# Layer A's attention of a two-layer diffusion trunk: three pairs of PSUM banks in turn, one bank for projections and one for values

## The chip, the cores and the metric

The kernel runs on one core of one Trainium2 chip. A core has a matrix engine (PE, with its weight loads PEld), three engines for elementwise work (DVE, ACT, POOL), a queue engine for transfers (SP), and PSUM, the memory that PE writes its results into: 8 banks of 512 float32 for each of the 128 partitions. A tile of 1024 float32 takes two banks, called a pair here. The metric is the device time of one execution in microseconds (us); lower is better.

## What is computed

Two layers over 1024 latent tokens (on a grid 64 wide) and 256 context tokens, each token a vector of 1024. The context tokens share the layer's weights. Layer 0 uses windowed attention with 16 query heads on 4 key heads of 64, a sink logit per head and a rotary embedding; layer 1 uses attention over a two-dimensional neighbourhood with a relative bias. Each has a gate path:

```python
for i in range(DEPTH):
    shift, scale, gate = split(silu(c) @ w_ada[i] + b_ada[i], 3)      # and the same for the context
    u  = h * (1 + scale) + shift
    uc = hc * (1 + scale_c) + shift_c
    if i == 0: y, yc = mixer_a(u, uc, ...)
    else:      y, yc = mixer_b(u, uc, ...)
    h = layer_norm(ALPHA * h + gate * y)          # hc likewise, after layer 0
# mixer_a
q, k, v, g = split(u @ w_in)                      # q, k rotated on the latent tokens
s_lat = where(|i - j| <= 128, q k^T / 8, -1e30)   # a block of 128 queries sees 3 blocks of keys
s_ctx = q kc^T / 8                                # and the 256 context keys
p = softmax([s_lat, s_ctx, sink])
y = ((p_lat v + p_ctx vc) * silu(g)) @ w_out
```

Context queries see the context keys only.

## The kernel before

Matrices are multiplied as 32-bit floats split into a high and a low part (three matmuls for a product). The program goes through layer A's modulated inputs, keys and values, then layer A's attention with its query and gate projections, the output projection and the layer norm, and then the same for layer B. The part that the change touches is layer A's attention.

**Sub-steps.** The 16 heads go in 8 pairs, p = 0 to 7. For each p there are 10 blocks b of 128 tokens (8 latent, 2 context) and two heads h: 160 sub-steps, k = 20p + 2b + h (`subsA`). Sub-step k computes its scores S_A (`qkA`, L694: PE L704 and L705, 640 columns for an inner block, 512 for blocks 0 and 7, 256 for the context blocks 8 and 9, each twice, with the high and the low part of the keys). DVE takes them out of PSUM with the mask and the row minimum (L317), POOL adds the sink (L322), ACT takes the exponent (L324). In the next sub-steps DVE takes the reciprocal of the sum (L328), POOL scales (L329), PE transposes the tile into T_A (L336, up to five times 128x128), ACT copies the high part out (L340) and DVE subtracts to get the low part (L342). After both heads of a block PE multiplies with the values into pvA (`pvA_fn`, L725, PE L733), first with the high part, one sub-step later with the low part; the result of two blocks stands in one bank, and after the second of them ACT (L742) and DVE (L743) take it out.

**Projections beside it.** While p is attended, the gates of p and the queries of p+1 are projected (`proj_pieces`, L190): for each of three chunks of tokens (512, 512 and 256) a tile pj of 24 matmuls (L208 to L210). A query chunk is taken out by DVE's shuffle (L469) and multiply by the cosine (L470), both of which read the bank, followed by POOL L471 and DVE L472 and by the copies L659 on ACT and L660 on DVE; the third chunk, of context tokens, goes to L659 and L660 at once. A gate chunk is taken out by ACT's tanh (L277) and DVE's L278. `merge` (L284) lays the two lists, attention and projection, into one another by their costs. DVE also works through products for the modulation of later stages (L611, L617).

**Order.** The framework builds each engine's order when the program is built, by simulating the engines: an instruction's priority is its place in the program, raised by `lift` for some (the eviction of the scores by 80, L342 by 60), and an instruction whose tile has no free bank is passed over until one is free. So the banks that a tile may take shape the order on all engines.

**Banks.** One pool for the whole kernel: two pairs (`psbig`, L97), which scores and transposes share, and four single banks (`psone`, L100), which all else shares: projections, values, transposes of the inputs, and the first output tiles yA0. A new tile waits until the last reader of the tile that held the bank has finished.

**The end of the stage.** In period p = 7 there are no further queries to project. In their place stand the splitting of the output weights and, from `og_first` on, the first output block's product into yA0, of two single banks. Behind the attention a loop over 10 blocks forms the output, the gate, the residual and the norm (L890).

Of the kernel before, what the change touches and what calls it, by code (L numbers as in the profile page):

```python
# [11 lines left out]
F32 = mybir.dt.float32  # L12
# [4 lines left out]
PSUM = bass.MemoryType.PSUM  # L17
DRAM = bass.MemoryType.DRAM

P = 128  # L20
# [62 lines left out]
def build(tc, i, out):  # L83
# [3 lines left out]
    es = ExitStack()  # L87
# [4 lines left out]
        return p, st  # L92

    dr = es.enter_context(tc.tile_pool(name="dr", bufs=1, space=DRAM))
    ps = es.enter_context(tc.tile_pool(name="ps", bufs=1, space=PSUM))

    def psbig(name):  # L97
        return ps.tile([P, 1024], F32, tag="big", bufs=2, name=name)

    def psone(name):  # L100
        return ps.tile([P, 512], F32, tag="one", bufs=4, name=name)

    cp = es.enter_context(tc.tile_pool(name="cp", bufs=1, side="left"))
    ident = cp.tile([P, P], F32, name="ident")
# [299 lines left out]
    HALVES = (slice(0, 512), slice(512, 1024))  # L404
# [239 lines left out]
    pp_st.close()  # L644
    pq, pq_st = pool("attA", "right")


    qA, gA, kA, vA = {}, {}, {}, {}

# [160 lines left out]
    for p in range(8):  # L810
        att = [x for row in rowsA[p * 20 : (p + 1) * 20] for x in row]
        if p % 2 == 0 and p:
            k_load(p // 2, 1)
        if p % 2 == 1 and p < 7:
            att.insert(20, (0.0, lambda p=p: k_load(p // 2 + 1, 0), 0))
            att.insert(24, (0.0, lambda p=p: v_loadA(p // 2 + 1), 0))
        if p < 7:
            n = len(att)
            for g in range(SEG[p]):
                att.insert(3 + g * (n // SEG[p] + 1), dots.pop(0))  # L820
            if not dots:
                att.append((0.0, dots_end, 0))
            merge(att, gprojA(p) + qprojA(p + 1), lead=0.0)
        else:

            att += [x for row in rowsA[8 * 20 :] for x in row]
            g7, fill = gprojA(7), []
            woA = OutWeights(up, "woA")
            for n, piece in enumerate(g7):
                fill.append(piece)  # L830
                if n >= 8:
                    fill.append((200.0, lambda j=n - 8: wo_piece(woA, i["wAo"], j)))
            assert len(fill) == G7_AT[2]
            oA0, yA0 = [], []

            def og_first():
                oA0.extend(og_small(og_load(0, 0)))
                yA0.extend(psone(f"yA0_{nh}") for nh in range(2))

            fill.append((0.0, og_first))  # L840
            for n in range(2 * KT):
                fill.append((300.0, lambda n=n: out_part(yA0, HALVES[n // KT], oA0, woA, (n % KT,))))
            merge(att[:-6], fill, lead=1500.0)
            gts = up.tile([P, 2, D], F32, tag="l2", bufs=1, name="gates")
            for v in range(2):
                gate_rows(gts[:, v], dcol[:, 0:8, v])
            raw = og_load(0, 1)
            merge(att[-6:], [])
# [42 lines left out]
    for b in range(10):  # L891
        z = oa.tile([P, D], F32, tag="z", bufs=2, name="z")
        dma(z, i["htok"][b])
        if b == 0:
            yh = yA0
        else:
            o = og_split(up, raw, "h2") if b % 2 else og_split(oa, raw, "og")
            if b < 9:
                raw = og_load(0, b + 1)
            y = psbig(f"yA{b}")  # L900
            yh = [y[:, sl] for sl in HALVES]
            for sl in HALVES:
                out_part(yh, sl, o, woA, range(KT))
        if pend is not None:
            u_from(*pend)
        g = gts[:, b // 8]
        for sl, yy in zip(HALVES, yh) if b == 0 else ((slice(0, D), y),):
            nc.vector.tensor_tensor(yy, yy, g[:, sl], ALU.mult)
            nc.vector.scalar_tensor_tensor(z[:, sl], z[:, sl], ALPHA, yy, ALU.mult, ALU.add)
        st = oa.tile([P, 2, 6], F32, tag="stat", bufs=2, name="stat")  # L910
        for nh in range(2):
            nc.vector.bn_stats(st[:, nh, :], z[:, HALVES[nh]])
        mv, rs = ln_stats(oa, st)
        nc.vector.scalar_tensor_tensor(rs[:, 0:1], mv[:, 0:1], -1.0, rs[:, 1:2], ALU.mult, ALU.mult)
        nc.scalar.activation(z, z, AF.Identity, bias=rs[:, 0:1], scale=rs[:, 1:2])
        if b < 8:
            dma(zdd[b * P : (b + 1) * P, :], z)
        pend = (b, z)

    def k_evac(dst, pl):  # L920
        def evac(pt, t0, n):
# [236 lines left out]
    def grid_rows(t, b):  # L1158

        return t.rearrange("(r c) d -> r c d", c=64)[:, 8 * b : 8 * b + 8, :]  # L1160
# [40 lines left out]
    for j in range(4):  # L1201
        t = ob.tile([P, D], F32, name=f"vec{j}")
# [4 lines left out]
    for b in range(8):  # L1207
        x = ob.tile([P, D], F32, tag="x", bufs=2, name="x")
        dma(x, grid_rows(zdd, b))  # L1209
        tok = slice(b * P, (b + 1) * P)  # L1210
        if 0 < b < 7:
            raw = og_load(1, b + 1, 7)
            on = og_split(ob, raw, "og") if b % 2 == 0 else og_split(ub, raw, "l2")
        nc.gpsimd.tensor_tensor(x, x, vecs[0], ALU.mult)  # L1214
        nc.gpsimd.tensor_tensor(x, x, vecs[1], ALU.add)  # L1215
        y = [y0, y1][b] if b < 2 else [psone(f"yB{b}_{nh}") for nh in range(3 if b == 7 else 2)]
        pairs = (o1 if b < 2 else o) + [(o7[:, 0, tok], o7[:, 1, tok])]

        cuts = (0, 512, 768, 1024) if b == 7 else (0, 512, D)
        parts = [slice(*c) for c in zip(cuts, cuts[1:])]  # L1220
        for sl in parts:
            out_part(y, sl, pairs, woB, range(KT) if b > 1 else (KT - 1,))
        if b:
            o = on
        if b == 0:
            g1 = ob.tile([P, D], F32, name="g1")
            gate_rows(g1, dcol[:, 24:32, 0])
        z = ob.tile([P, D], F32, tag="z", bufs=3, name="z")
        st = ob.tile([P, 3, 6], F32, tag="stat", bufs=2, name="stat")
        for j, sl in enumerate(parts):  # L1230
            nc.vector.tensor_tensor(z[:, sl], part_of(y, sl), g1[:, sl], ALU.mult)  # L1231
            nc.vector.tensor_tensor(z[:, sl], z[:, sl], x[:, sl], ALU.add)  # L1232
            nc.vector.bn_stats(st[:, j, :], z[:, sl])  # L1233
        mv, rs = ln_stats(ob, st[:, : len(parts)])
        cuts = (0, 512, 1024) if b == 7 else (0, D)
        parts = [slice(*c) for c in zip(cuts, cuts[1:])]
        for sl in parts:
            nc.vector.scalar_tensor_tensor(z[:, sl], z[:, sl], mv[:, 0:1], vecs[2][:, sl], ALU.subtract, ALU.mult)  # L1238
        for sl in parts:
            nc.vector.scalar_tensor_tensor(z[:, sl], z[:, sl], rs[:, 1:2], vecs[3][:, sl], ALU.mult, ALU.add)  # L1240
            dma(grid_rows(out, b)[:, :, sl], z[:, sl])
    ob_st.close()
    ub_st.close()
    wp_st.close()
# [94 lines left out]
```

## Time and profile before

| | |
|---|---|
| time, median of 3 runs | 1449.96 us (1449.54 to 1451.34) |
| time of the profiled execution | 1450.25 us |
| its span, first to last instruction | 1448.5 us |
| granted PE clock, mean | 0.994 |
| PE, DVE, ACT, POOL busy | 96%, 68%, 51%, 44% of the span |
| layer A's attention | about 97.8 to 590 us of the span |
| one p within it | about 60.7 us |

The profile is one execution taken by the hardware profiler. The profiled execution's own time is 1.75 us above its span. "L336" is a line of the kernel. In a list of waits, "PE T_A L336 <- DVE m_A L317" is time in which PE stood before a transpose until DVE had done its work at L317. A row of a timeline gives start, duration, engine, line, operation, and what is written from what is read; PE's matmuls are pipelined, so that a row's duration is longer than the distance to the next one.

### The profile page before, as it was taken

Reading aid. Unit: us, or ns where it says so; the run is one execution under the profiler, and the core shown is the slowest. Engines: PE = TensorE matmul, PEld = TensorE weight load, DVE = VectorE, ACT = ScalarE, POOL = GpSimd, SP = SyncE. Lnnn points to the kernel's source line nnn. Section 1 sums busy time; section 2 is a strip of 40 time slices with the busy share of each in tenths; the row PEclk is TensorE's granted clock in tenths of the full one; section 3 lists DMA queues with packets and bytes.
Section 4 is the critical chain, followed back from the end, with each engine's and each line's share of the span. In section 5 each row is a group of like instructions: output and inputs, shape, how many; then the busy total and the mean of one; then the engine's idle time right before and its main releaser. Section 6 shows DMA issues by size and latency. Waiting matters only on the chain. (4 is left out here: it accounts for less than half of the span.)

```text
span 1448.5 us, 25148 instructions
## 1 busy us (share of the span) xinstructions
PE 1393.6 (96%) x8815; PEld 1217.2 (84%) x8816; DVE 988.8 (68%) x2216; ACT 733.9 (51%) x1561; POOL 631.7 (44%) x779
## 2 busy tenths in 40 slices
PE   8998999999999999999999999999999999998995
PEld 5887888888888888788888899888988898887775
DVE  4658887878888789566423766555565565667698
ACT  4336776677676778332222545554454444557310
POOL 0326666666666657233301333333233333336664
PEclk9999999999999999999999999999999999999998
DMA  9472114123222124434278565565555564384353
GB/s 369 172 227 85 60 48 131 45 77 101 68 70 62 56 67 131 133 129 136 75 216 230 156 195 152 150 166 146 168 147 152 146 182 140 102 207 151 114 133 93
DMA packets 117229, 195.05 MB, mean 135 GB/s; under 512 B 9328, under 2 KB 57840, under 8 KB 117104
## 3 DMA queue, kind: packets, MB, share of 16 engines
q1 hardware_dynamic: 117104, 193.45, 44.4%
q8 instruction: 70, 1.15, 0.3%
q14 instruction: 55, 0.45, 0.1%
HBM read 141.51 MB, written 51.90 MB: 134 GB/s over the span
## 5 line engine op out<-in xcount | busy, mean ns | idle before, releaser
L329 POOL TENSOR_SCALAR s_B<-s_B,rs_B 128x640 f32<-128x640 f32 (+1 forms) x128 | 101.1, 790 | 298.0 <-DVE rs_B L328 243.9
L208 PE MATMUL pj<-uBh,wh 128*128 128x512 f32 (+1 forms) x448 | 176.0, 393 | 0.0
L209 PE MATMUL pj<-uBl,wh 128*128 128x512 f32 (+1 forms) x448 | 170.3, 380 | 0.0
L210 PE MATMUL pj<-uBh,wl 128*128 128x512 f32 (+1 forms) x448 | 170.1, 380 | 0.0
L324 ACT ACTIVATE s_B<-s_B,m_B 128x640 f32<-128x640 f32 (+1 forms) x128 | 102.9, 804 | 131.2 <-DVE m_B L317 131.1
L324 ACT ACTIVATE s_A<-s_A,m_A 128x641 f32<-128x641 f32 (+2 forms) x160 | 119.5, 747 | 88.7 <-DVE m_A L317 73.7
L164 POOL TENSOR_TENSOR wl<-wr,wh 128x512 fp32r<-128x512 f32 x64 | 87.7, 1370 | 162.1 <-ACT wh L162 139.8
L329 POOL TENSOR_SCALAR s_A<-s_A,rs_A 128x640 f32<-128x640 f32 (+2 forms) x160 | 126.8, 793 | 58.0 <-DVE rs_A L328 55.7
L317 DVE CUSTOM_DVE_ANT_0 s_A<-S_A,msk,nsk 128x640 f32<-128x640 f32 (+2 forms) x160 | 123.6, 774 | 34.1 <-PE S_A L705 17.7
L342 DVE TENSOR_TENSOR pt_B<-T_B,pt_B 128x640 fp32r<-128x640 f32 (+1 forms) x128 | 100.9, 788 | 61.0 <-ACT pt_B L340 60.6
L208 PE MATMUL pj<-uAh,wh 128*128 128x512 f32 (+1 forms) x384 | 140.0, 365 | 0.0
L209 PE MATMUL pj<-uAl,wh 128*128 128x512 f32 (+1 forms) x384 | 137.8, 359 | 0.0
L210 PE MATMUL pj<-uAh,wl 128*128 128x512 f32 (+1 forms) x384 | 137.5, 358 | 0.0
L342 DVE TENSOR_TENSOR ptl_A<-T_A,pth_A 128x640 fp32r<-128x640 f32 (+2 forms) x160 | 114.0, 713 | 15.3 <-PE pvA L733 7.1
L336 PE MATMUL T_A<-ident,s_A 128*128 128x128 f32 x672 | 101.1, 275 | 12.2 <-DVE m_A L317 8.9
L336 PEld LDWEIGHTS T_A<-ident,s_A 128*128 128x128 f32 x672 | 77.2, 140 | 40.2 <-issue 16.7
L340 ACT CAST pt_B<-T_B 128x640 fp32r<-128x640 f32 (+1 forms) x128 | 84.3, 658 | 47.6 <-PE T_B L336 46.6
L317 DVE CUSTOM_DVE_ANT_0 s_B<-S_B,bias 128x640 f32<-128x640 f32 (+1 forms) x128 | 100.4, 784 | 10.5 <-PE S_B L1036 9.7
L340 ACT CAST pth_A<-T_A 128x640 fp32r<-128x640 f32 (+2 forms) x160 | 96.4, 603 | 16.8 <-PE T_A L336 14.1
L210 PEld LDWEIGHTS pj<-uBh,wl 128*128 128x128 f32 x448 | 84.3, 188 | 16.6
L336 PE MATMUL T_B<-ident,s_B 128*128 128x128 f32 x608 | 88.7, 275 | 9.9 <-DVE pt_B L342 5.0
L242 PE MATMUL pv<-wh,uBh 128*128 128x256 f32 x320 | 92.8, 291 | 3.1 <-ACT wh L162 3.1
(219 smaller groups left out, 3883.6 us busy)
## 6 DMA issues: line engine op xcount, KB each, us to landing
kB<-kdB SPq DMA_DIRECT2D x64, 320.0 KB, 5.2
gw<-in_wadaT SPq DMA_DIRECT2D x48, 256.0 KB, 2.8
vdB<-st SPq DMA_DIRECT2D x20, 512.0 KB, 3.2
vB<-vdB SPq DMA_DIRECT2D x16, 640.0 KB, 4.7
wada<-in_wadaC SPq DMA_DIRECT2D x16, 512.0 KB, 9.6
kdB<-st SPq DMA_DIRECT2D x16, 512.0 KB, 3.0
qdB<-st SPq DMA_DIRECT2D x16, 512.0 KB, 3.5
qB<-qdB SPq DMA_DIRECT2D x32, 256.0 KB, 4.7
```

Source lines behind the costliest of these rows:

```text
L164: e.tensor_tensor(lo, r, f32(hi), ALU.subtract)
L208: mm(pt[:, :n], hi[:, sl], rh, start=kt == 0, stop=False)
L209: mm(pt[:, :n], hi[:, sl], rl, start=False, stop=False)
L210: mm(pt[:, :n], lo[:, sl], rh, start=False, stop=kt == KT - 1)
L242: mm(pt, lh, hi[:, sl], start=kt == 0, stop=False)
L317: nc.vector.tensor_tensor_reduce(outp, sc, in1, scale, init if init is not None else 3e38, ALU.add, ALU.min, accum_out=s.m)
L324: nc.scalar.activation(s.t[:, :n], s.t[:, :n], AF.Exp, bias=s.m, scale=-1.0, accum_out=s.sum)
L329: nc.gpsimd.tensor_scalar(s.t[:, : s.w], s.t[:, : s.w], s.rs, 1.0, ALU.mult, ALU.mult)
L336: nc.tensor.transpose(tp[:, k * P : (k + 1) * P], s.t[:, src * P : (src + 1) * P], ident)
L340: nc.scalar.copy(pt.hi[:, :n, hl, :], tv)
L342: nc.vector.tensor_tensor(pt.lo[:, :n, hl, :], tv, f32(pt.hi[:, :n, hl, :]), ALU.subtract)
```

## The change

The banks are handed out by a small class with three stages. Up to the values' projection: two pairs and four single banks, as before. In layer A's attention: three pairs under three names, which scores and transposes take in turn, in program order, by a counter; one single bank for tiles whose name begins with "pj" and one for those that begin with "pv". After the first output block: two pairs and four single banks again. In `og_first`, the first output tile takes the third pair, and scores and transposes go on with the other two. The pools are opened so that a bank is handed on tile by tile. No instruction is added, removed or resized; lines stand 15 lower after the first part of the diff, and 18 lower behind the second.

```diff
--- before.py
+++ after.py
@@ -92,13 +92,28 @@
         return p, st
 
     dr = es.enter_context(tc.tile_pool(name="dr", bufs=1, space=DRAM))
-    ps = es.enter_context(tc.tile_pool(name="ps", bufs=1, space=PSUM))
-
-    def psbig(name):
-        return ps.tile([P, 1024], F32, tag="big", bufs=2, name=name)
-
-    def psone(name):
-        return ps.tile([P, 512], F32, tag="one", bufs=4, name=name)
+
+    class Banks:
+
+
+        def open(self, name, pairs, ones):
+            self.st = ExitStack()
+            self.ps = self.st.enter_context(tc.tile_pool(name=name, bufs=1, space=PSUM, reuse_waits="tile"))
+            self.pairs, self.ones, self.n = list(range(pairs)), ones, 0
+
+        def big(self, name):
+            t = self.pairs[self.n % len(self.pairs)]
+            self.n += 1
+            return self.ps.tile([P, 1024], F32, tag=f"big{t}", bufs=1, name=name)
+
+        def one(self, name):
+            if self.ones == 4:
+                return self.ps.tile([P, 512], F32, tag="one", bufs=4, name=name)
+            return self.ps.tile([P, 512], F32, tag=name[:2], bufs=1, name=name)
+
+    banks = Banks()
+    banks.open("ps0", 2, 4)
+    psbig, psone = banks.big, banks.one
 
     cp = es.enter_context(tc.tile_pool(name="cp", bufs=1, side="left"))
     ident = cp.tile([P, P], F32, name="ident")
@@ -643,6 +658,9 @@
     merge([], vproj_pieces(-1, uA, v_evac(pp, vdA), 2))
     pp_st.close()
     pq, pq_st = pool("attA", "right")
+
+    banks.st.close()
+    banks.open("psA", 3, 2)
 
 
     qA, gA, kA, vA = {}, {}, {}, {}
@@ -835,7 +853,9 @@
 
             def og_first():
                 oA0.extend(og_small(og_load(0, 0)))
-                yA0.extend(psone(f"yA0_{nh}") for nh in range(2))
+                banks.pairs = [0, 1]
+                y = banks.ps.tile([P, 1024], F32, tag="big2", bufs=1, name="yA0")
+                yA0.extend(y[:, sl] for sl in HALVES)
 
             fill.append((0.0, og_first))
             for n in range(2 * KT):
@@ -916,6 +936,9 @@
         if b < 8:
             dma(zdd[b * P : (b + 1) * P, :], z)
         pend = (b, z)
+        if b == 0:
+            banks.st.close()
+            banks.open("psB", 2, 4)
 
     def k_evac(dst, pl):
         def evac(pt, t0, n):
@@ -1239,6 +1262,7 @@
         for sl in parts:
             nc.vector.scalar_tensor_tensor(z[:, sl], z[:, sl], rs[:, 1:2], vecs[3][:, sl], ALU.mult, ALU.add)
             dma(grid_rows(out, b)[:, :, sl], z[:, sl])
+    banks.st.close()
     ob_st.close()
     ub_st.close()
     wp_st.close()
```

What this does to the order. Names: S_A36 and T_A36 are the score and the transposes of sub-step 36, pj16_1 is chunk 1 of the projection whose first weight tile is 16 (the queries of p = 2), pvA1_4 the values of p = 1 from block 4 on; the last number of a name is that of the buffer.

First place: the end of the period of p = 1, where the last rows of pj16_1, the short sub-steps 36 to 39 and the third chunk pj16_2 meet. PE before:

```order
L336 MATMUL T_A34_2563<-ident_63,s_A34_2468 128x128 x4
L705 MATMUL S_A37_2570<-kA0_0_975,qA3_1647 128x256
L705 MATMUL S_A37_2570<-kA0_1_978,qA3_1647 128x256
L208 MATMUL pj16_1_2449<-uAh1_106,wh17_1873 128x512
L209 MATMUL pj16_1_2449<-uAl1_109,wh17_1873 128x512
L210 MATMUL pj16_1_2449<-uAh1_106,wl17_1874 128x512
L733 MATMUL pvA1_4_2478<-ptl_A30_2396,vA0_981 128x256 x5
L208 MATMUL pj16_2_2604<-uAh2_107,wh16_1869 128x256
L209 MATMUL pj16_2_2604<-uAl2_110,wh16_1869 128x256
L210 MATMUL pj16_2_2604<-uAh2_107,wl16_1870 128x256
L336 MATMUL T_A35_2610<-ident_63,s_A35_2504 128x128 x4
```

PE now:

```order
L225 MATMUL pj16_1_2453<-uAh1_106,wl17_1878 128x512
L723 MATMUL S_A37_2574<-kA0_0_979,qA3_1651 128x256
L723 MATMUL S_A37_2574<-kA0_1_982,qA3_1651 128x256
L751 MATMUL pvA1_4_2482<-ptl_A30_2400,vA0_985 128x256 x5
L351 MATMUL T_A35_2614<-ident_63,s_A35_2508 128x128 x4
L723 MATMUL S_A38_2624<-kA0_0_979,qA2_1650 128x256
L723 MATMUL S_A38_2624<-kA0_1_982,qA2_1650 128x256
L351 MATMUL T_A36_2653<-ident_63,s_A36_2545 128x128 x2
L723 MATMUL S_A39_2661<-kA0_0_979,qA3_1651 128x256
L723 MATMUL S_A39_2661<-kA0_1_982,qA3_1651 128x256
L351 MATMUL T_A37_2707<-ident_63,s_A37_2577 128x128 x2
L223 MATMUL pj16_2_2608<-uAh2_107,wh16_1873 128x256
```

Before, pj16_2 begins behind one group of values, ahead of T_A35. Now all of its rows come behind S_A39 and T_A37, and between the last row of pj16_1 and the first of pj16_2 there is only attention.

DVE at the same place, from the eviction of S_A36 on. Before:

```order
L317 ISA s_A36_2541,m_A36_2542<-S_A36_2538,msk_141,nsk_142 128x256
L317 ISA m_A36_2542 128x1
L342 TENSOR_TENSOR ptl_A32_2490<-T_A33_2524,pth_A32_2489 128x5x128
L328 RECIPROCAL rs_A36_2544<-sum_A36_2543 128x1
L617 ISA gj_2535,dcol_71<-gw_2533,gh_1148 128x512
L617 ISA dcol_71 128x1
L317 ISA s_A37_2573,m_A37_2574<-S_A37_2570,msk_141,nsk_142 128x256
L317 ISA m_A37_2574 128x1
L469 STREAM_SHUFFLE rb_2584<-pj16_1_2449 128x512
L342 TENSOR_TENSOR ptl_A34_2562<-T_A34_2563,pth_A34_2561 128x4x128
L328 RECIPROCAL rs_A37_2576<-sum_A37_2575 128x1
L470 TENSOR_TENSOR ra_2583<-pj16_1_2449,cos_139 128x512
```

Now:

```order
L484 STREAM_SHUFFLE rb_2588<-pj16_1_2453 128x512
L332 ISA s_A37_2577,m_A37_2578<-S_A37_2574,msk_141,nsk_142 128x256
L332 ISA m_A37_2578 128x1
L357 TENSOR_TENSOR ptl_A34_2566<-T_A34_2567,pth_A34_2565 128x4x128
L343 RECIPROCAL rs_A36_2548<-sum_A36_2547 128x1
L357 TENSOR_TENSOR ptl_A34_2566<-T_A35_2614,pth_A34_2565 128x4x128
L332 ISA s_A38_2627,m_A38_2628<-S_A38_2624,msk_141,nsk_142 128x256
L332 ISA m_A38_2628 128x1
L343 RECIPROCAL rs_A37_2580<-sum_A37_2579 128x1
L332 ISA s_A39_2664,m_A39_2665<-S_A39_2661,msk_141,nsk_142 128x256
L332 ISA m_A39_2665 128x1
L485 TENSOR_TENSOR ra_2587<-pj16_1_2453,cos_139 128x512
```

The shuffle and the multiply (L469 and L470, now L484 and L485) are the two readers of pj16_1. Before, two rows stood between them. Now there are the evictions of S_A37, S_A38 and S_A39 with their reads of the row minimum, both subtractions of T_A34 and T_A35 and two reciprocals.

Second place: PE around score 30, in the middle of the same period. Before:

```order
L704 MATMUL S_A30_2295<-kA0_0_975,qA2_1646 128x384
L705 MATMUL S_A30_2295<-kA0_0_975,qA2_1646 128x256
L704 MATMUL S_A30_2295<-kA0_1_978,qA2_1646 128x384
L705 MATMUL S_A30_2295<-kA0_1_978,qA2_1646 128x256
L208 MATMUL pj16_0_2281<-uAh0_105,wh16_1869 128x512
L209 MATMUL pj16_0_2281<-uAl0_108,wh16_1869 128x512
L210 MATMUL pj16_0_2281<-uAh0_105,wl16_1870 128x512
L733 MATMUL pvA1_2_2310<-pth_A24_2139,vA0_981 128x256 x5
L208 MATMUL pj16_0_2281<-uAh0_105,wh16_1869 128x512
L209 MATMUL pj16_0_2281<-uAl0_108,wh16_1869 128x512
L210 MATMUL pj16_0_2281<-uAh0_105,wl16_1870 128x512
L336 MATMUL T_A28_2329<-ident_63,s_A28_2201 128x128 x5
```

Now:

```order
L351 MATMUL T_A28_2333<-ident_63,s_A28_2205 128x128
L722 MATMUL S_A30_2299<-kA0_0_979,qA2_1650 128x384
L723 MATMUL S_A30_2299<-kA0_0_979,qA2_1650 128x256
L722 MATMUL S_A30_2299<-kA0_1_982,qA2_1650 128x384
L723 MATMUL S_A30_2299<-kA0_1_982,qA2_1650 128x256
L351 MATMUL T_A28_2333<-ident_63,s_A28_2205 128x128 x4
L351 MATMUL T_A29_2366<-ident_63,s_A29_2246 128x128 x5
L722 MATMUL S_A31_2341<-kA0_0_979,qA3_1651 128x384
```

Before, seven rows of projection and values stood between the score S_A30 and T_A28, and T_A29 came later still. Now the last four transposes of T_A28 and all of T_A29 follow the score at once; T_A29 takes the pair that S_A30 had.

## The prediction

> **What bounds the kernel now.** I read the page first, then the busy time by stage, then the waits of PE in the attention stage, then the timelines of PE and DVE at those waits.
>
> ```profile
> span 1448.5 us, 25148 instructions
> PE 1393.6 (96%) x8815; PEld 1217.2 (84%) x8816; DVE 988.8 (68%) x2216; ACT 733.9 (51%) x1561; POOL 631.7 (44%) x779
> ```
>
> PE is busy for 96% of the span; DVE, second, for 68%. The change adds no matmul, so the time can fall by no more than the idle time of PE, and rises by what PE waits more. Busy time by stage (columns: stretch, its length, then busy time and count for PE, PEld, DVE, ACT and POOL, clock, DMA share, GB/s):
>
> ```profile
> core 0: us, PE busy (x) PEld busy (x) DVE busy (x) ACT busy (x) POOL busy (x), PEclk, DMA share, GB/s
> 0.00:97.80 97.80, 94.15 (x764) 76.34 (x766) 54.37 (x105) 37.62 (x76) 18.60 (x18) 1.00 0.71 257
> 97.80:590.00 492.20, 472.17 (x3062) 413.13 (x3061) 402.25 (x970) 345.22 (x779) 318.46 (x457) 1.00 0.26 81
> 590.00:1450.00 860.00, 827.24 (x4993) 727.74 (x4991) 532.13 (x1142) 351.05 (x706) 294.59 (x305) 0.99 0.53 151
> ```
>
> The middle row is the stage that the change is about: layer A's attention with its projections. PE idles there for 492.20 - 472.17 = 20.0 us, and DVE is busy for 402 of 492 us (82%). So PE leads, but DVE, which empties nearly every PSUM bank, is close behind. The waits of PE in that stage (us in total, times, longest):
>
> ```profile
> engine line waited for: us in total, times, longest us
> PE T_A L336 <- DVE m_A L317: 8.9, 16, 1.6
> PE S_A L704 <- DVE ptl_A L342: 5.1, 7, 1.2
> PE S_A L705 <- DVE ptl_A L342: 1.8, 6, 0.3
> ```
>
> These are the waits for a pair of banks: a transpose waits until DVE has read the scores that held the pair (8.9), a score waits until DVE has read a transposed tile (5.1 + 1.8). Together they are 15.8 us, and 15.8 is all that a third pair could win. No wait for a bank of the projections (pj) or of the values (pvA) stands in the answer: with four single banks there was none worth a row. One such wait, on PE and then on DVE:
>
> ```profile
> 303.00 0.28 PE L210 MATMUL pj<-uAh,wl 128*128 128x256 f32 x1
> 303.82 0.46 PE L704 MATMUL S_A<-kA,qA 128*128 128x384 f32 x1 [0.54 <-DVE ptl_A L342]
> ```
>
> ```profile
> 301.15 0.88 DVE L317 CUSTOM_DVE_ANT_0 s_A<-S_A,msk,nsk 128x640 f32<-128x640 f32 x1
> 301.96 0.08 DVE L317 DVE_READ_ACCUMULATOR2_ANT m_A<- 128x1 f32 x1
> 302.95 0.82 DVE L342 TENSOR_TENSOR ptl_A<-T_A,pth_A 128x640 fp32r<-128x640 f32 x1
> 303.68 0.15 DVE L328 RECIPROCAL rs_A<-sum_A 128x1 f32<-128x1 f32 x1
> 303.75 0.67 DVE L278 SCALAR_TENSOR_TENSOR gA<-th,pj 128x512 f32<-128x512 f32 x1
> 304.33 0.82 DVE L342 TENSOR_TENSOR ptl_A<-T_A,pth_A 128x640 fp32r<-128x640 f32 x1
> ```
>
> The subtraction ends at 302.95 + 0.82 = 303.77 and the score starts 0.05 us later.
>
> **Prices.** DVE starts an instruction before the last one has ended, so I price by the distance between starts: a score's eviction (L317) of 640 columns 301.96 - 301.15 = 0.81, the subtraction at L342 of 640 columns 303.68 - 302.95 = 0.73, L278 0.58. The other shapes:
>
> ```profile
> 210.57 0.47 DVE L317 CUSTOM_DVE_ANT_0 s_A<-S_A,msk,nsk 128x256 f32<-128x256 f32 x1
> 210.98 0.08 DVE L317 DVE_READ_ACCUMULATOR2_ANT m_A<- 128x1 f32 x1
> 210.98 0.01 DVE L469 LOAD_MASK_SELECT rb<-pj  x1
> 210.98 0.75 DVE L469 STREAM_SHUFFLE rb<-pj 128x512 f32<-128x512 f32 x1
> 211.63 0.67 DVE L342 TENSOR_TENSOR ptl_A<-T_A,pth_A 128x512 fp32r<-128x512 f32 x1
> 212.22 0.15 DVE L328 RECIPROCAL rs_A<-sum_A 128x1 f32<-128x1 f32 x1
> 212.29 0.67 DVE L470 TENSOR_TENSOR ra<-pj,cos 128x512 f32<-128x512 f32 x1
> ```
>
> That is 0.41 for an eviction of 256 columns, 0.64 for the shuffle, 0.60 for L342 at 512 columns, 0.08 for a reciprocal, 0.67 for L470. On PE:
>
> ```profile
> 262.12 0.28 PE L705 MATMUL S_A<-kA,qA 128*128 128x256 f32 x1
> 262.24 0.28 PE L704 MATMUL S_A<-kA,qA 128*128 128x256 f32 x1
> 263.17 0.75 PE L733 MATMUL pvA<-pth_A,vA 128*128 128x256 f32 x5
> 263.76 0.39 PE L208 MATMUL pj<-uAh,wh 128*128 128x512 f32 x1
> 263.99 0.39 PE L209 MATMUL pj<-uAl,wh 128*128 128x512 f32 x1
> 264.45 0.71 PE L336 MATMUL T_A<-ident,s_A 128*128 128x128 f32 x5
> 264.92 0.36 PE L704 MATMUL S_A<-kA,qA 128*128 128x256 f32 x1
> 265.12 0.28 PE L705 MATMUL S_A<-kA,qA 128*128 128x256 f32 x1
> ```
>
> A matmul of 256 columns takes 262.24 - 262.12 = 0.12, one of 512 0.23, five of the values 0.59; five transposes and one 256 take 265.12 - 264.45 = 0.67, so a transpose 0.11. The latency from PE to DVE and back:
>
> ```profile
> 200.87 0.28 PE L705 MATMUL S_A<-kA,qA 128*128 128x256 f32 x1
> ```
>
> ```profile
> 201.30 0.75 DVE L317 CUSTOM_DVE_ANT_0 s_A<-S_A,msk,nsk 128x512 f32<-128x512 f32 x1 [0.29 <-PE S_A L705]
> ```
>
> The matmul's slot ends at 200.87 + 0.12 = 200.99, DVE starts 0.31 later; the end of an instruction overhangs its slot by 0.09 (0.82 - 0.73), and PE follows 0.05 later: 0.45 in all.
>
> **How I count.** For each reuse of a bank I set two sums against each other. The slack is what PE issues, in its order, between the last matmul into the old tile and the first into the new one. The need is what stands on DVE from then up to the old tile's last reader, plus the latency. PE waits for need minus slack, less the waits that already stand between the two. I did this for every reuse from the first projection of the stage to its last value matmul. For the kernel before the waits add up to 5.2 us with a latency of 0.3, 10.9 with 0.45, 20.5 with 0.6 and 33.1 with 0.75; the windows show 20.0. So I take 0.6, and the 0.15 above the measured 0.45 stands for what the count leaves out (ACT's and POOL's share in the chains).
>
> **The change, part by part.** *Third pair.* The order says who follows whom in a pair. Before, a pair alternates: score k comes after transposes k-4, and transposes k after score k+2. With three pairs taken in turn, score k still comes after transposes k-4; only the transposes move back by one sub-step, to score k+1. So the 6.9 us of scores that wait keep their partner, and only the 8.9 of transposes gain distance. And PE's order shifts with it: in the places of the section on the change, transposes 29 now stand directly behind transposes 28, with score 30, whose pair they take, just ahead. Their slack is four transposes, 0.44; the need 0.81 + 0.6 = 1.41; a wait of 0.97, where before projection matmuls stood. Summed over the stage, the waits for pairs do not fall but go from 20.5 to 25.8 (12.2 transposes behind scores, 11.6 scores behind transposes, 2.0 their own kind).
>
> *One bank for projections.* A chunk must now be read out before the next begins. Median slack between chunks is 10 to 12 us before and 2.2 now. The readers are two on DVE (shuffle L469, multiply L470), or ACT's tanh and L278. In the odd periods (p = 1, 3, 5) the tail of the period is the place quoted, the two short blocks of 256 columns. After the last matmul of pj16_1 PE has S_A37 0.24, the values 0.59, T_A35 0.44, S_A38 0.24, T_A36 0.22, S_A39 0.24, T_A37 0.22: 2.2 us. DVE has, before the bank is free, evictions 36 to 39 (4 x 0.41), the shuffle 0.64, two L342 (1.20), two reciprocals (0.15) and the multiply 0.67: 4.30. The lifted evictions of the scores that ran ahead stand in front of the multiply. With 0.6 the tail waits 2.7 in all, spread over S_A38 1.20, S_A39 0.23, T_A37 0.32 and pj16_2 0.98. Walked event by event with 0.45, the same tail waits 2.35. Before, pj16_2 had a bank of its own and filled this very place.
>
> *One bank for values.* pvA is reused every two blocks; slack falls from about 13 to 4.1 us, need 3.8 + 0.6 at the start of a period (0.3) and 5.86 + 0.6 less 1.26 already waited in the even tail (0.8).
>
> *Sum.* An odd period: 0.07 + 0.32 + 0.97 + 0.57 + 2.73 + 0.97 = 5.6. An even one: 0.07 + 0.32 + 0.97 + 0.57 + 0.28 + 0.90 + 0.08 + 0.78 + 0.61 = 4.6. The first q projection, where PE has nothing else to do between chunks 0 and 1 (slack zero, 1.31 + 0.6 = 1.9) and the first rows: 4.7. Period 0 3.5, periods 1 to 6 together 30.0, period 7 with its tail 6.7. That is 44.9 us after against 20.5 before: **+24.4**. By kind: projections +14.2, values +4.9, pairs +5.3.
>
> *The rest.* From the first output block on the order is the same but for a few rows, and two pairs and four single banks are back: 0. The bound for closing the pool there is one reading of a y half with the next transposes behind it, 0 to 2 us; nothing covers it but the output matmuls of block 1. Against the profiled execution's own 1450.25: 1450.25 + 24.4 = 1474.7; that stands 0.3 above the median shown, 1449.96. I say 1475.
>
> The rule of the Trainium skill that speaks against this change is in "Perfetto Trace Analysis", Optimizing Tensor Performance, Matmuls: independent matmul groups should rotate through different banks, so that one's evacuation overlaps the next one's matmuls. One bank for the projections gives that up among themselves. If no attention work covered it, each of the 47 reuses would expose its readers' 0.64 + 0.67 and the latency, 47 x 1.9 = 90 us; the rows' slack covers all but 14.2 of it.
>
> **The rivals.** *Faster: the pair waits go.* The mechanism: transposes really find their pair free (median slack behind scores 1.7 before, 3.7 now), DVE then never falls behind, and the scores stop waiting too. Then -15.8, and of the new waits only those without any latency remain, 8.1 for projections and 3.0 for values: 1450.25 - 15.8 + 11.1 = 1445.6; 1434.5 if those hide as well. It decides where projections and values wait less than 15.8 together. For it: the median. Against it: the partner of the scores is unchanged, and the places with slack 0.44. The Trainium skill has the rule for it ("Perfetto Trace Analysis", Optimization Strategy): a gap that repeats on the engine that should be saturated can mean too little SBUF or PSUM for the next tile; the rows agree that such gaps repeat each period.
>
> *A swap.* The count without any latency gives 20.7 after, as much as the 20.0 measured: 1451. This is also what comes out if the third pair changes nothing in who waits and the new waits replace the old. Against it: without latency the count gives only 1.8 before.
>
> *A smaller loss.* Latency 0.3 for the new waits, 31.2 - 20.0: 1461.5.
>
> *A larger loss.* Latency 0.75: 53.0 - 20.0 gives 1483; where DVE stands one subtraction (0.60) further back at 16 of the 47 projection reuses, 9.6 more, 1493.
>
> **How the numbers follow.** Forecast 1475 (own range 1465 to 1482) 0.62; smaller loss 0.12; larger 0.08; faster 0.12; swap 0.06. Leaving out the faster rival and the swap leaves out 0.18, so the range is 1455 to 1493. 0.2% (3 us) is about what a measurement of this kernel can tell from no change. Faster 0.12, same 0.06, slower 0.82.
>
> **What would show it.** PE idle in the attention stage near 45 instead of 20 us, the stage about 25 longer, PE's busy time there still 472; in the waits new rows of pj behind DVE's ra and gA (about 14), of pvA behind otmp (about 5); the rows T_A behind m_A and S_A behind ptl_A still there, together over 15; about 2.5 us of waits at the end of each odd period; the stretch from the first output block on as long as before. I am wrong if T_A and S_A rows nearly vanish, if no pj row comes up, or if the last stretch differs by more than 2 us.

## The result and the profile after

The changed kernel takes 1501.75 us (median of 4 runs, 1500.8 to 1504.8) against 1449.89 for the kernel before on the same chip: a ratio of 1.0359, 95% interval 1.0341 to 1.0377. It is slower by 52 us; 25 were forecast, and the range ended at 1493. The page of the changed kernel begins so:

```profile
span 1500.5 us, 25154 instructions
PE 1418.4 (95%) x8816; PEld 1229.8 (82%) x8816; DVE 994.5 (66%) x2216; ACT 734.5 (49%) x1561; POOL 628.8 (42%) x779
```

With the same matmuls PE is busy for 1418.4 instead of 1393.6 us. So as the profile counts it the loss has two parts: PE idles more, and the time in which it counts as busy grows. The busy time of the kernel before in layer A's attention, from the first query projection to the last value matmul, and in the rest behind it, with the columns of the prediction's windows:

```profile
80.00:588.50 508.50, 488.47 (x3148) 427.30 (x3148) 413.11 (x990) 351.98 (x794) 323.80 (x460) 1.00 0.28 86
588.50:1450.00 861.50, 828.74 (x5000) 729.00 (x4998) 532.37 (x1143) 351.42 (x707) 295.33 (x306) 0.99 0.52 151
```

And of the changed kernel:

```profile
80.00:641.00 561.00, 510.90 (x3152) 440.47 (x3151) 415.73 (x990) 351.67 (x794) 320.58 (x460) 0.98 0.26 78
641.00:1502.00 861.00, 830.64 (x5004) 728.79 (x5002) 535.82 (x1143) 352.45 (x707) 295.06 (x305) 0.99 0.53 151
```

The whole loss lies in the first of the two stretches, which grows from 508.5 to 561.0. In it PE idles for 561.00 - 510.90 = 50.1 us instead of 20.0 (+30.1), and is busy for 22.4 us more. The last stretch is the same. The waits of PE from 80 us to the end of that stage (total, times, longest):

```profile
PE T_A L351 <- POOL s_A L344: 12.5, 19, 1.4
PE S_A L722 <- DVE ptl_A L357: 8.9, 10, 1.3
PE pvA L751 <- DVE otmp L761: 8.4, 10, 2.2
PE pj L223 <- DVE ra L485: 6.5, 4, 5.7
PE T_A L351 <- DVE m_A L332: 6.4, 10, 0.8
PE S_A L723 <- DVE ptl_A L357: 3.7, 7, 0.9
```

The third pair did shorten the waits of transposes for a pair (m_A, 8.9 before, 6.4 now). But the scores wait longer than before (8.9 + 3.7 for 5.1 + 1.8), pvA and pj now wait, and the largest row is new and concerns no bank: transposes that wait until POOL has scaled their own s.

**The first projection.** PE and DVE of the changed kernel where chunk 1 of the first query projection waits for the one bank:

```profile
87.10 0.39 PE L225 MATMUL pj<-uAh,wl 128*128 128x512 f32 x1
93.14 0.79 PE L223 MATMUL pj<-uAh,wh 128*128 128x512 f32 x1 [5.65 <-DVE ra L485]
...
94.15 0.63 PE L225 MATMUL pj<-uAh,wl 128*128 128x512 f32 x1
94.58 0.63 PE L223 MATMUL pj<-uAh,wh 128*128 128x512 f32 x1
...
99.52 0.39 PE L223 MATMUL pj<-uAh,wh 128*128 128x512 f32 x1
99.75 0.39 PE L224 MATMUL pj<-uAl,wh 128*128 128x512 f32 x1
```

```profile
90.56 0.42 DVE L281 SCALAR_TENSOR_TENSOR st<-pv-1_4_908,st 128x256 fp32r<-128x256 f32 x1 [1.71 <-ACT st L280]
91.44 0.42 DVE L281 SCALAR_TENSOR_TENSOR st<-pv-1_4_908,st 128x256 fp32r<-128x256 f32 x1 [0.45 <-ACT st L280]
91.79 0.72 DVE L484 STREAM_SHUFFLE rb<-pj 128x512 f32<-128x512 f32 x1
92.41 0.68 DVE L485 TENSOR_TENSOR ra<-pj,cos 128x512 f32<-128x512 f32 x1
```

The two readers of the bank stand on DVE behind the evacuations of the values (L281). DVE itself is idle most of that time: these wait for ACT, and ACT for the store of an earlier st tile:

```profile
90.15 0.38 ACT L280 ACTIVATE st<-pv-1_4_908 128x256 fp32r<-128x256 f32 x1 [1.75 <-DMA vdA<-st]
```

Behind the 5.65 us of idle time PE issues a matmul of 512 columns every 0.43 us (94.58 - 94.15) instead of 0.23, until about 99.

**The granted clock.** All 5 us windows of the stage in which it was below 1.00:

```profile
90.00:95.00 5.00, 1.86 (x4) 1.49 (x5) 2.76 (x6) 1.14 (x3) 1.40 (x2) 0.74 0.69 231
95.00:100.00 5.00, 5.00 (x15) 3.89 (x14) 1.37 (x2) 0.85 (x2) 0.00 (x0) 0.57 1.02 231
105.00:110.00 5.00, 3.79 (x20) 3.79 (x21) 4.75 (x9) 4.05 (x10) 3.53 (x4) 0.66 1.10 263
160.00:165.00 5.00, 3.35 (x20) 2.37 (x19) 4.19 (x14) 3.14 (x9) 4.36 (x8) 0.91 0.18 52
165.00:170.00 5.00, 5.00 (x34) 5.00 (x34) 4.26 (x11) 3.11 (x7) 2.40 (x4) 0.75 0.02 3
365.00:370.00 5.00, 4.72 (x27) 4.55 (x26) 4.83 (x9) 3.32 (x8) 4.10 (x5) 0.66 0.85 197
435.00:440.00 5.00, 3.31 (x14) 3.05 (x15) 4.50 (x10) 2.22 (x7) 4.03 (x5) 0.72 0.40 102
440.00:445.00 5.00, 5.00 (x29) 4.28 (x28) 2.11 (x6) 2.41 (x7) 1.10 (x3) 0.94 0.02 7
```

PE's busy time in each (second number) times what is missing from 1.00 adds up to 8.3 us: an estimate of what the lower clock took. In the kernel before, the clock was 1.00 in each of the prediction's windows up to 590 us.

**The tail of an odd period.** PE and POOL at the first place of the section on the change, in p = 1:

```profile
227.50 0.60 PE L351 MATMUL T_A<-ident,s_A 128*128 128x128 f32 x4
228.61 0.50 PE L723 MATMUL S_A<-kA,qA 128*128 128x256 f32 x2 [0.51 <-DVE ptl_A L357]
229.56 0.44 PE L351 MATMUL T_A<-ident,s_A 128*128 128x128 f32 x2 [0.45 <-POOL s_A L344]
229.75 0.48 PE L723 MATMUL S_A<-kA,qA 128*128 128x256 f32 x2
230.82 0.44 PE L351 MATMUL T_A<-ident,s_A 128*128 128x128 f32 x2 [0.58 <-POOL s_A L344]
231.53 0.39 PE L223 MATMUL pj<-uAh,wh 128*128 128x256 f32 x1 [0.28 <-DVE ra L485]
```

```profile
227.66 1.27 POOL L486 TENSOR_TENSOR rb<-rb,sin 128x512 f32<-128x512 f32 x1 [0.72 <-DVE rb L484]
228.88 0.18 POOL L337 COPY s_A<-nsk 128x1 f32<-128x1 f32 x1
229.03 0.47 POOL L344 TENSOR_SCALAR s_A<-s_A,rs_A 128x256 f32<-128x256 f32 x1
```

PE runs through the attention rows one behind the other, with no projection between them, and waits before each of four. The transposes at 229.56 wait for the scaling at 229.03, which stood on POOL behind 1.27 us of the rotation of pj16_1. POOL is only the last to come there: the reciprocal that the scaling needs starts on DVE at 228.47, so a free POOL could have begun some 0.4 us sooner and no more. The distance of starts less the usual issue time gives 0.67, 0.71, 0.83 and 0.49 for the four, 2.70 us together, where the idle column shows 1.82. A wait costs some 0.2 more than its row says: the matmul before it counts as busy for its whole row (0.28 us for 256 columns), though the next one can start after 0.12.

For the comparisons below I use that distance: from 82 us to the last value matmul, the distances of PE's starts less 0.228, 0.178, 0.1185 or 0.109 us for 512, 384, 256 and 128 columns. This lost time is 39 us before and 92 after, 53 more, so it accounts for the whole difference. Counted from the single matmul records of the traces it is 41 and 93.

### The profile page after: what moved, and what is told of

Same layout as the page of the kernel before. It is cut to its first block, busy times and chain, and to the rows that moved or that the text cites. A ratio compares the mean times of both kernels' runs of the same rounds, so it can differ in the third digit from the quotient of the medians.

```text
span 1500.5 us, 25154 instructions
## 1 busy us (share of the span) xinstructions
PE 1418.4 (95%) x8816; PEld 1229.8 (82%) x8816; DVE 994.5 (66%) x2216; ACT 734.5 (49%) x1561; POOL 628.8 (42%) x779
## 5 line engine op out<-in xcount | busy, mean ns | idle before, releaser
L223 PE MATMUL pj<-uAh,wh 128*128 128x512 f32 (+1 forms) x384 | 145.2, 378 | 7.2 <-DVE ra L485 6.5
L351 PE MATMUL T_A<-ident,s_A 128*128 128x128 f32 x672 | 103.2, 276 | 19.3 <-POOL s_A L344 12.5
L722 PE MATMUL S_A<-kA,qA 128*128 128x384 f32 (+1 forms) x256 | 85.6, 356 | 10.4 <-DVE ptl_A L357 8.9
```

Of the source, the lines that this page charges most:

```text
L223: mm(pt[:, :n], hi[:, sl], rh, start=kt == 0, stop=False)
L351: nc.tensor.transpose(tp[:, k * P : (k + 1) * P], s.t[:, src * P : (src + 1) * P], ident)
L722: mm(sc[:, 512 - n : 512], ql, kk[:, t0 : t0 + n], start=l == 0, stop=l == 1)
```

## The experiments

Each ratio is to the kernel before, run on the same chip in the same batch.

**e1: the single banks without the third pair.**

```diff
-            t = self.pairs[self.n % len(self.pairs)]
-            self.n += 1
-            return self.ps.tile([P, 1024], F32, tag=f"big{t}", bufs=1, name=name)
+            return self.ps.tile([P, 1024], F32, tag="big", bufs=2, name=name)
```

> The attention stage has two pairs, either of which any score or transpose may take (as before the change), but one bank for the projections and one for the values (as after it); two banks stand empty until the first output tile takes them. Theory A (the single banks cost the time: the projections lose their second bank, so PE has nothing to put between the rows of attention): at least 40 of the 52 us stay, 1490 us or more. Theory B (the third pair in fixed turn costs it, since a row must wait for the pair that its number gives it): 1450 to 1465 us.

1507.57 us, ratio 1.0418 (1.0397 to 1.0440). Theory A holds: the whole loss, and a little more, is there without the third pair. (A part of it at the start of the stage comes with the opening of the pool, which e1 has too; see e4.) The waits for a pair are now larger:

```profile
PE T_A L349 <- DVE m_A L330: 19.2, 16, 4.5
PE pj L221 <- DVE ra L483: 6.4, 4, 5.7
PE pvA L749 <- DVE otmp L759: 5.6, 9, 1.6
...
PE T_A L349 <- POOL s_A L342: 1.0, 1, 1.0
```

The third pair takes the transposes' wait from 19.2 to 6.4 and gives them one for POOL of 12.5 (1.0 in e1). What it wins in the end is the difference of the two ratios, 0.6%; their intervals do not overlap.

**e2: two single banks for both.**

```diff
-            return self.ps.tile([P, 512], F32, tag=name[:2], bufs=1, name=name)
+            return self.ps.tile([P, 512], F32, tag="one", bufs=2, name=name)
```

> Three pairs in turn as after the change, but projections and values share the two single banks, either may take either. Theory A, if what counts is that a chunk may begin in the second bank before the first is read out: 1470 to 1485 us. Theory B: no change against the changed kernel, 1497 to 1505 us. A third reading (two single banks are too few, however they are named): 1497 us or more too; e1 tells that from B.

1494.16 us, ratio 1.0330 (1.0304 to 1.0356). In microseconds that lies between the first two ranges, but the kernel before was 3 us faster in this batch: the ratio applied to 1449.89 gives 1497.7, in the range of theory B and of the third reading, and its interval overlaps that of the changed kernel (1.0341 to 1.0377). So the times alone do not show a gain. The trace of the profiled execution, the fastest of the four, has a lost time of 82 instead of 92 us, 6 of the 10 at the start, where chunk 1 waits less for a bank:

```profile
PE pj L223 <- DVE st L281: 1.7, 1, 1.7
...
PE pj L223 <- DVE ra L485: 1.4, 4, 0.5
```

(The row behind ra was 6.5.) So the division by name is at most a small part; that there are two in place of four is the large one, as e4 shows below.

**e3: the first projection with four banks.** The pool is opened behind it:

```diff
     merge([], qprojA(0))
+    banks.st.close()
+    banks.open("psA", 3, 2)
```

> The changed kernel, but the pool with the single banks is opened behind the first query projection, which so still has four single banks. The trace of the changed kernel shows PE idle for 5.65 us between its chunks 0 and 1 and then at a granted clock of 0.57 to 0.74 for some 5 us. If that is a loss of its own: 8 to 10 us faster than the changed kernel, about 1492 us, the idle row gone and the clock at 1.00 there. If the attention behind it only waits for the same DVE work a little later: within 3 us of 1502.

1498.57 us, ratio 1.0350 (1.0328 to 1.0371), which the interval doesn't tell from 1.0359. The second expectation holds: the ratio applied to 1449.89 gives 1500.6. The idle row is gone, but another comes up, and the clock falls behind that:

```profile
PE S_A L719 <- DVE qA L675: 4.3, 1, 4.3
```

```profile
100.00:105.00 5.00, 4.26 (x15) 3.71 (x16) 0.61 (x2) 0.00 (x0) 0.00 (x0) 0.66 1.12 322
```

The first score needs the rotated queries, and these come hardly sooner: it starts at 100.74 us, in the changed kernel at 101.56. So the 5.65 us were for the most part not a loss of their own.

**e4: a control, three pools with the banks of before** (`psA` with two pairs of either kind and four singles, yA0 in singles).

```diff
-    banks.open("psA", 3, 2)
+    banks.open("psA", 2, 4)
```

> A control: three pools one after another as in the changed kernel, each with two pairs (any of the two) and four single banks as before the change. If handing the banks from pool to pool costs nothing: 1447 to 1453 us. If the hand-over itself costs (a drain at each opening): 1455 us or more, with new waits of PE near the first score and behind the first output block.

1462.42 us, ratio 1.0102 (1.0081 to 1.0122). The hand-over costs something here:

```profile
PE yA L432 <- DVE z L925: 8.0, 1, 8.0
...
PE S_A L720 <- DMA kA<-kdA: 5.7, 2, 3.1
```

The 8.0 us stand at the opening of the last pool, where block 1's output waits until block 0 is done. The changed kernel doesn't have this wait, so it is the control's own. (Why is open: e5 has it with 7.3 us, but e6, whose yA0 lies in single banks too, does not.) From 113 us to the last value matmul e4's lost time is 36 us, before 38: in the stage itself the pools cost nothing. Ahead of it they do. From 82 to 113 us the lost time is about 1 us in the kernel before, 9 in e4, 8 in e3 and 14 in the changed kernel. So of the 13 us that the changed kernel loses more at the start, some 8 are there with four single banks as well, once the pool is opened at this place, and only some 5 need the one bank for projections. In e4 PE comes to the first score, behind 3 matmuls of the next projection, before its keys have landed and stands still until 98.83 us; in the kernel before there are 14 such matmuls, which last until the first score at 98.12.

**e5 and e6: which single bank.** As e4, with three banks for projections and one for values, and the reverse.

```diff
+            tag = "pv" if name[:2] == "pv" else "pj"
+            return self.ps.tile([P, 512], F32, tag=tag, bufs=1 if tag == "pv" else 3, name=name)
```

> As the control e4 (two pairs, any of the two; three pools), but of the four single banks three are for projections and one for values, in the attention stage. Theory A1 (the one projection bank is what costs): at most 10 us over the control, so a ratio of 1.010 to 1.017 to the kernel before. Theory A2 (the one bank for values costs as much, since its reader on DVE stands far back): 20 to 35 us over the control, 1.024 to 1.034, with 8 us or more of waits of pvA behind otmp.

> The counterpart: one bank for projections, three for values. Theory A1: 30 to 45 us over the control e4, a ratio of 1.031 to 1.042, with the 5.65 us at the first projection and no waits of pvA. Theory A2: 10 to 25 us over the control, 1.017 to 1.028.

e5 1478.88 us, 1.0210 (1.0189 to 1.0231); e6 1483.36, 1.0236 (1.0211 to 1.0261). e6 lies in the range of theory A2 and e5 between the two ranges; the 8 us of waits of pvA forecast for e5 came out as 5.6. Neither theory holds alone. In lost time from 113 us on, with the control's 36 and without e5's own output wait of 7.5: one bank for values 52 (+16), one for projections 60 (+25), both (e1) 81 (+45). The two losses nearly add.

**e7: any of the three pairs.** One name with three buffers in place of the turn.

> The changed kernel with the three pairs under one name, so that a tile takes whichever comes free instead of the one whose turn it is. If the fixed turn holds rows back: 10 us or more faster than the changed kernel, a ratio of 1.029 or less. If the single banks set the loss, as e1, e5 and e6 say: within 5 us of it, 1.032 to 1.040.

1508.24 us, ratio 1.0412 (1.0399 to 1.0426): slower than the changed kernel and just above the second range, as with two pairs (e1). The fixed turn isn't what costs; it is what lets the third pair win its little.

**e8: the readers of the single banks first on DVE and ACT.**

```diff
+            with lift(200):
                 nc.vector.stream_shuffle(b, pt, SWAP)
                 nc.vector.tensor_tensor(a, pt, cos[:, t0 : t0 + n], ALU.mult)
...
+                with lift(200):
                     nc.scalar.copy(tmp[hs], pv[64:128, :, h, :])
                     nc.vector.tensor_tensor(tmp[hs], pv[0:64, :, h, :], tmp[hs], ALU.add)
```

(and the gate's tanh and product)

> The changed kernel with the priority of the readers of the single banks raised by 200 (shuffle, cosine multiply, tanh and the gate's product, and both instructions that take out pvA), above the 80 of the scores' evictions. If the place of these readers behind lifted evictions on DVE is what holds the single banks: waits of pvA under 3 instead of 8.4 us, and 10 to 20 us faster than the changed kernel, a ratio of 1.022 to 1.029. If the loss lies in PE's order itself (a chunk that cannot begin leaves no filler, whoever stands first on DVE): within 5 us of it, 1.032 to 1.039.

1489.75 us, ratio 1.0282 (1.0257 to 1.0307): some 11 us faster than the changed kernel. The place behind lifted evictions is a real part, though not the larger one:

```profile
PE T_A L352 <- POOL s_A L345: 11.0, 15, 1.6
PE pj L223 <- DVE ra L487: 10.0, 6, 6.8
...
PE pvA L753 <- DVE otmp L764: 3.6, 4, 1.8
```

pvA's waits behind otmp fall from 8.4 to 3.6, not quite to the 3 expected; the transposes' wait for POOL stays, and the projections' waits behind ra are longer than before (10.0 for 6.5).

**e9: scores four sub-steps ahead.**

```diff
-AHEAD_A, LIFT_A = 3, 80
+AHEAD_A, LIFT_A = 4, 80
...
-        s.t = pl.tile([P, 641], F32, tag="s", bufs=3, name=f"s_{name}")
+        s.t = pl.tile([P, 641], F32, tag="s", bufs=4 if name[0] == "A" else 3, name=f"s_{name}")
```

> The changed kernel with scores four sub-steps ahead of their transposes instead of three, and the fourth buffer for s that this needs (room for it: one buffer instead of two for the products of the modulation, and otmp shares the buffer of the rotation). The changed kernel's new wait of transposes for POOL's scaling of their own s (12.5 us) is gone where the softmax chain simply needs one more sub-step of lead: that row under 4 us, and 8 to 15 us faster, a ratio of 1.025 to 1.031. If the lead is taken back by scores that wait longer for their pair: the row S_A behind ptl_A rises from 12.6 to 20 us or more, and the ratio stays at 1.032 or more.

1513.13 us, ratio 1.0450 (1.0419 to 1.0480). Of the first expectation the wait for POOL came out and the time did not; of the second the ratio came out, but by other waits than the scores' (3.8 + 1.3 behind ptl_A instead of 12.6):

```profile
PE T_A L351 <- DVE m_A L332: 14.0, 11, 1.8
PE pvA L751 <- DVE otmp L761: 12.7, 18, 1.9
...
PE T_A L351 <- POOL s_A L344: 2.3, 5, 0.9
```

The wait for POOL is gone (12.5 to 2.3), and more comes back as waits for pairs and for the values' bank. The edits that made room may have a share in that: the single buffer for the modulation's products, and otmp in the rotation's buffer, which could itself hold back the readers of pvA. They weren't tried apart, so e9 shows what happens to the wait for POOL and not what one more sub-step of lead is worth.

**e10: e2 and e8 together.**

> The changed kernel with both remedies that won something: projections and values share the two single banks (e2), and the readers of these banks are raised by 200 (e8). If the two gains add: e2 lost 4 us less in the stage than the changed kernel and 6 less at its start, e8 14 less in the stage; together some 20 us faster than the changed kernel, a ratio of 1.020 to 1.024. If both relieve the same wait: not better than e8 alone, 1.027 or more. In no case below 1.010, since two single banks remain.

1480.71 us, ratio 1.0228 (1.0210 to 1.0245), lost time 69 us. That is faster than e8 by more than the intervals, and in the range of the first expectation: the gains add. It is the best version with a third pair that was run, and still 2.3% behind the kernel before.

**e11 and e12: the kernel before, with DVE's order changed.** e11 takes e8's edit; e12 this:

```diff
-        with lift(60 if a else 0):
+        with lift(100 if a else 0):
```

> The kernel before, with the same readers raised by 200. With four single banks nothing waits for these readers (slack 10 us and more), so lifting them can win nothing: 0.998 to 1.002 if their place on DVE is free, 1.002 to 1.010 if the scores' evictions that they now pass are late by that.

> The kernel before, with the subtraction that frees a transposed tile (L342) raised by 100 instead of 60, so above the scores' evictions (80). Its waits of scores behind ptl_A (6.9 us) should fall under 3. If DVE's order is what sets those waits: 3 to 6 us faster, 0.996 to 0.998. If the time only moves to the transposes behind the scores' evictions (8.9 us before, then 12 or more): 0.999 to 1.004.

e11 1455.69 us, 1.0050 (1.0038 to 1.0062), in the second range: with four single banks these readers are better left behind the scores. The new waits are not those behind the scores' evictions, though (the row behind m_A falls to 5.2), but of transposes behind ptl_A (6.3) and behind POOL (3.5). e12 1446.86 us, 0.9995 (0.9985 to 1.0004), not told from no change. Neither wait moved as expected: its row of transposes behind m_A falls from 8.9 to 3.3, while the scores' waits stay (4.7 + 3.4 for 5.1 + 1.8) and 2.9 of transposes behind ptl_A come up. No version that was run beats the kernel before.

## Why the prediction was too small

- **The step that failed** is in the first part: "The change adds no matmul, so the time can fall by no more than the idle time of PE, and rises by what PE waits more", and with it "PE's busy time there still 472". PE's idle time rose by 30.1 us, near the 24.4 forecast; but PE's busy time rose by 22.4, which stood in no term and in no rival. Of it some 8 are the granted clock. Another 5 are the restarts: the view of the waits lists 63 instead of 34, and each costs about 0.16 beyond its row, as 303.82 against 303.00 in the prediction's own fence shows (a distance of 0.82, less 0.12 for the matmul, against 0.54). Some 9 us are spread over distances without a row. About 3 of them are the second matmul behind a wait, which starts late too (104.32 us behind 104.03 in the changed kernel: 0.29 for 384 columns instead of 0.178); where the rest comes from stays open.
- The latency of 0.6 was fitted to an idle time of 20.0, while by the distance of starts the kernel before lost 39 us in the stage. So what a wait costs beyond its idle row had no place in the count.
- **The first projection** was priced at 1.9 us, from DVE's own work. It was 5.65 and then the lower clock. What stood before the bank's readers was waiting for ACT and a store, which the count didn't follow. The opening of the pool at this place was priced at nothing; by e4 it holds some 8 of the 13 us that the start lost.
- **Transposes behind their own data** had no term of their own: 12.5 us. The count knows a bank's reuse only, and the 0.15 added to the latency was all that stood for ACT and POOL. Where the transposes moved up in PE's order the bank is no longer what comes last; POOL's scaling is. e1 and e9 show it from both sides: without the third pair 1.0 us, with one more sub-step of lead and a fourth buffer for s 2.3.
- **The tail of the odd periods** came out at 2.70 us against 2.7 in p = 1, but that is luck: 2.70 is the distance of starts, 1.82 the idle time to which the count was fitted, and two of the four waits are POOL's, where the prediction put them on banks. T_A29's wait, forecast at 0.97, took 0.75 of idle time:

```profile
203.35 0.74 PE L351 MATMUL T_A<-ident,s_A 128*128 128x128 f32 x5 [0.75 <-DVE m_A L332]
```

- **By kind**, idle time forecast and found: projections 14.2 and 7.2, of which 5.65 at the start, and none behind gA; values 4.9 and 8.4; scores behind transposes 11.6 and 12.6; transposes behind scores 12.2 and 6.4. That the total of the idle time came near was luck: parts that were too large made up for the one that was missing. (The terms written out for periods 1 to 6 also add up to 30.6, not to the 30.0 in the sum.)
- **The pairs:** that the scores keep their partner and their waits don't fall held; they rose. That one bank each loses more than a third pair gains held too, and e1, e5 and e6 show it. The bank rule quoted from the Trainium skill ("Perfetto Trace Analysis", Optimizing Tensor Performance, Matmuls) is borne out: with the rotation over four banks taken away, the stage loses 45 us (e1 against e4).
- **The rest:** the last stretch is as long as before, as forecast.

## What to carry to other kernels

Call a filler the work that PE does while other engines' chains run, here the projections. Before a bank is taken from a filler, ask what PE has to do while it can't begin: here a wait for one bank pulled the filler out of the places where it hid other engines' chains, and those chains then stood bare. Price a new stall by the distance of starts, not by its idle row, and add what the clock loses behind it. A buffer that removes one wait shows its worth only where the next thing to come last, here the data itself, is early enough.

## What the runs showed of the hardware

After 5.65 us without a matmul PE ran at about half its rate for some 6 us. In e3 a wait of 4.3 us was followed by a granted clock of 0.66. In the changed kernel the clock also fell at 106, 164, 365 and 437 us, where no single wait was above 1.9 us; yet between 300 and 305 us, with PE busy for 2.46 of 5.00 us, it stayed at 1.00:

```profile
300.00:305.00 5.00, 2.46 (x19) 2.02 (x18) 4.75 (x11) 2.98 (x9) 3.92 (x6) 1.00 0.25 57
```

So the same idle share of a window of 5 us is not always followed by a lower clock. The clock records of the traces show what decides here. In all fourteen runs the granted clock is either 1.00 or 0.50, and within a run it changes only at multiples of one step of 3.413 us. Per step, count what PE issued, each matmul with its usual issue time, from 80 us to the last value matmul. Of the steps at full clock, 48 were followed by half clock, and in none of them was PE busy by this count for more than 42%; 2106 were followed by full clock, and in none of them for less than 40%. In the changed kernel the steps that ended at 106, 164, 365 and 437 us held 30%, 39%, 28% and 39%; the one from 300.7 us held 42% and kept its clock. That a busy share of some 40% in one step is the threshold is an estimate from these counts. So two waits that fall into one step can cost the clock, and a wait of the same length that is shared between two steps need not.

The Trainium skill ("TensorE: Matmul & The Clock Gate", Part 1: The HAM clock gate) puts the threshold at about one idle window of 3.4 us, with half the clock until PE has been busy for as long again. The length of the step agrees, and so do the two long waits; the slow stretch behind the 5.65 us was two steps long, and PE began again within the first. But the steps before the other drops were not idle: there PE was busy for up to 42%, and in this the runs decide against the page's rule.
